# First weights of a transformer block loaded by k tile: one array of 520 columns in place of chunk loads

## The chip, the cores and the metric

The kernel runs on one core of a Trainium2 chip. Five engines work side by side, each through its own list of instructions in order: TensorE (PE in the profile, with PEld for its weight loads), VectorE (DVE), ScalarE (ACT), GpSimd (POOL) and SyncE (SP). They wait for each other by semaphores. SP issues nearly all DMA transfers; their data is moved by 16 DMA engines. The metric is the device time of one execution in microseconds, as a median of runs.

## The reference

One block: a projection of the normalized input into nine parts, a gated delta rule on four heads, dilated attention on eight heads, an output projection and a gated feed-forward part. S and D are 1024, all in float32.

```python
def reference(x, w_in, conv_w, a_log, dt_bias, onorm_g, rel_bias, w_out, ...):
    h = rmsnorm(x, g_mix_pre[l])
    proj = h @ w_in[l]
    qa, ka, va, gate_a, beta_a, alpha_a, qb, kb, vb = jnp.split(proj, split_at, axis=-1)
    out_a = gated_deltanet(qa, ka, va, gate_a, beta_a, alpha_a, ...)
    out_b = dilated_attention(qb, kb, vb, rel_bias)
    mix = jnp.concatenate([out_a, out_b], axis=-1) @ w_out[l]
    x = x + rmsnorm(mix, g_mix_post[l])
    h = rmsnorm(x, g_ffn_pre[l])
    f = (jax.nn.silu(h @ w_gate[l]) * (h @ w_up[l])) @ w_down[l]
    x = x + rmsnorm(f, g_ffn_post[l])
```

The change touches only the first product, `h @ w_in`, and of it the columns that are computed first: 128 columns of the first key head, 128 of the first query head, 256 of the attention's values (`vb`), and the eight of beta and alpha.

## The kernel before

**Products in three terms.** Every float32 matrix is split into a high half, rounded to the format that PE multiplies fast (`fp32r`), and the low half that is left. A product is three matmuls: high by high, high by low, low by high (`mm3`, line 557). A split of weights is a CAST for the high half (ACT or DVE) and a subtraction, TENSOR_TENSOR, for the low half (DVE or POOL); it stands in `split_sb`, line 568. The input x comes transposed, in tiles of 128 of its 1024 features (a "k tile", 0 to 7) by 512 tokens. `prep_xt` (line 1384) multiplies it by the gain `gT`: ACT makes the high half `hTh`, DVE then makes the low half `hTl`.

**The first projection.** `proj_first` (line 755) runs for the first 512 tokens (`hf` 0) tile by tile over k, as its data comes: for each k tile six matmuls of 512 columns for the two chunks (into two PSUM banks named `pj`) and twelve of 264 columns for the values with beta and alpha (four token tiles, banks named `tp`). For k tiles 0 and 1 the three terms are ordered so that those with `hTl` come late. For the second 512 tokens it runs the two chunks alone, and `proj_v` adds the values. A chunk is 128 columns of `w_in` in an array `[chunk, 128, k tile, 128]`; chunk 4 is the first key head, 0 the first query head, 24 and 25 hold the values (256 columns for four k tiles each), so that a k tile of one chunk is a row of 512 bytes in each partition.

**The loads.** `load_w` (line 653) issues on SP, in this order: the gain, k tile 0 of both chunks (64 KB each), `w_ba` (all of beta's and alpha's weights, 32 KB), the values of k tile 0 (128 KB), x of k tile 1 (256 KB), k tile 1 of both chunks and of the values; then for each pair of k tiles the two chunks (128 KB each for two k tiles), x, and the values of each k tile. x of k tile 0 comes on ACT's own queue. Behind these come `ident`, the token rows `xn` (512 KB each, for the norms) and x for the second half of the tokens. Raw weights have four buffers (`rawS`), split weights sixteen (`wS`), x tiles six, token rows three. The DMA semaphores are eight, used in turn, so that an issue also waits until the transfer eight before it has landed.

**The order.** A scheduler in Python (`Weaver`, line 238) runs the parts of the kernel as strands, estimates times, and writes each engine's instructions in the order that it finds. Every instruction is issued from its line 287, which is why the profile shows L287 everywhere. `prep_w` (line 720) is the strand that splits the weights of one chunk; `ev_w` (line 715) names the event that tells `proj_first` that a k tile of a chunk is split. `norm_in` (line 1410) squares a token row on ACT into `ss`, and DVE and POOL make `rtok`, the factor of the norm, of it; PE then transposes `rtok` against `ident`, and `v_sink` (line 838) scales the finished values.

Of the kernel before, what the change touches and what calls it, by code (L numbers as in the profile page):

```python
# [21 lines left out]
P = 128  # L22
# [3 lines left out]
KT = D // P  # L26
# [517 lines left out]
def block_kernel(ctx: ExitStack, tc: tile.TileContext, a, out):  # L544
# [108 lines left out]
    def load_w():  # L653

        yield SY.dma_start(gT[:], a["g_mix_pre_t"])
        first = chunks(order[0]) + chunks(order[1])
        vs = chunks(order[2])
        got = {c: [] for c in first + vs}
        evs = {c: [[Event() for _ in range(2 + (c in first and not i))] for i in range(2)] for c in first + vs}
        for k in range(0, KT, 2):  # L660
            i, j = k // 4, k % 4
            for n, c in enumerate(first):
                if not j:
                    wr = yield rawS.get([P, 4, P], F32, name="wr")
                    got[c].append(wr)
                x = 2 if k else 1
                yield SY.dma_start(got[c][i][:, j:j + x, :], a["w_in"][c][:, k:k + x, :])
                evs[c][i][len(evs[c][i]) - 2 + j // 2 if k else 0].fire()
                if not k:
                    w.spawn(prep_w(c, got[c], evs[c]), 1)  # L670
                if k and not n:
                    yield from load_xt(k, 0)
            if not k:
                yield SY.dma_start(wba[:], a["w_ba"])
            c = vs[i]
            wr = yield rawS.get([P, 4, P], F32, name="wr")
            got[c].append(wr)
            for n in range(2):
                if n:
                    yield from load_xt(k + 1, 0)  # L680
                    for d in first if not k else ():
                        yield SY.dma_start(got[d][0][:, 1:2, :], a["w_in"][d][:, 1:2, :])
                        evs[d][0][1].fire()
                yield SY.dma_start(wr[:, 2 * n:2 * n + 2, :], a["w_in"][c][:, 2 * (j + n):2 * (j + n) + 2, :])
                evs[c][j // 2][n].fire()
                if not j and not n:
                    w.spawn(prep_w(c, got[c], evs[c]), 1)
        yield SY.dma_start(ident[:], a["c_ident"])
        for t in range(3):
            yield from load_x(t)  # L690
            yield from load_xt(t, 1)
        for k in range(3, KT):
            yield from load_xt(k, 1)
            if k == 4:
                yield from load_x(3)
        for t in range(4, NT):
            yield from load_x(t)
        ev_x.fire()
        for item in order[3:]:
            yield from load_item(item)  # L700

    def load_item(item):
        for c in chunks(item):
            z, evs = [], [[Event()] for _ in range(2)]
            for i in range(2):
                wr = yield rawS.get([P, 4, P], F32, name="wr")
                yield SY.dma_start(wr[:], a["w_in"][c][:, 4 * i:4 * i + 4, :])
                z.append(wr)
                evs[i][0].fire()
            w.spawn(prep_w(c, z, evs), 1)  # L710

    ev_x = Event()
    ev_wh = {(c, (i, j)): Event() for c in loaded for i in range(2) for j in range(3)}

    def ev_w(c, k):
        if c in (24, 25):
            return ev_wh[c, (k % 4 // 2, k % 2)]
        return ev_wh[c, (0, min(k, 2)) if k < 4 else (1, k % 4 // 2)]

    def prep_w(c, raw, got):  # L720
        hi, lo = [], []
        for i in range(4):
            if c in (24, 25):
                z = yield wS.get([P, 2, WB], F32R, name="w")
            else:
                z = yield wS.get([P, 4, P], F32R, name="w")
            (lo if i % 2 else hi).append(z)
        wts[c] = hi, lo
        for i, (wh, wl) in enumerate(zip(hi, lo)):
            yield got[i][0]  # L730
            wr = raw[i]
            if c in (24, 25):

                k = 4 * (c - 24) + 2 * i
                yield After(wba[:])
                yield from split_sb(wh[:, :, 256:], wl[:, :, 256:], wba[:, k:k + 2, :])
                wh, wl, wx = wh[:, :, 0:256], wl[:, :, 0:256], wr[:].rearrange("p (k x) c -> p k (x c)", x=2)
            else:
                wh, wl, wx = wh[:], wl[:], wr[:]
            for j, ev in enumerate(got[i]):  # L740
                yield ev
                n, m = wx.shape[1], len(got[i])
                x = slice(*((0, 1, 2, n)[j:j + 2] if m == 3 else (n // m * j, n // m * (j + 1))))
                x = (slice(None), x)
                yield After(wx[x], part=m > 1)
                if c == chunks(order[0])[0] and not i and not j:
                    yield V.tensor_copy(wh[x], wx[x])
                    yield V.tensor_tensor(wl[x], wx[x], wh[x].bitcast(F32), ALU.subtract)
                else:
                    yield from split_sb(wh[x], wl[x], wx[x])  # L750
                ev_wh[c, (i, j)].fire()
            rawS.put(wr)
        loaded[c].fire()

    def proj_first(hf, sinks):

        cs = chunks(order[0]) + chunks(order[1])
        ps = []
        for _ in cs:
            z = yield pj.get([P, 512], F32, name="pj")  # L760
            ps.append(z)
        vs = []
        if not hf:
            for t in range(4):
                z = yield pt.get([P, 4, P], F32, name="tp")
                vs.append(z)
        for k in range(KT):
            if vs and k < 2:
                for c in cs:
                    yield ev_w(c, k)  # L770
                yield ev_xt[k, hf]
                o0, o1 = (mm3(z[:], wh[0][:, k, :], wl[0][:, k, :], *h_of(k, 0, 512), k == 0, False)
                          for z, (wh, wl) in zip(ps, (wts[c] for c in cs)))
                yield [o0[0], o0[2], o1[0], o0[1], o1[1], o1[2]]
            for c, z in zip(cs, ps) if not vs or k > 1 else ():
                yield ev_w(c, k)
                yield ev_xt[k, hf]
                wh, wl = wts[c]
                yield mm3(z[:], wh[k // 4][:, k % 4, :], wl[k // 4][:, k % 4, :], *h_of(k, hf * 512, 512),
                          k == 0, k == KT - 1)  # L780
            if vs:
                yield ev_w(24 + k // 4, k)
                ops = [v_ops(0, t, v_rows(0, z), [k]) for t, z in enumerate(vs)]
                if k < 2:
                    yield [op for o in ops for op in (o[0], o[2])] + [o[1] for o in ops]
                else:
                    for o in ops:
                        yield o
        if hf:
            wS.slots = wS.slots[:8]  # L790
            for c in cs:
                wS.put(*wts[c][0], *wts[c][1])
# [132 lines left out]
        return t  # L925

    convw = const("convw", [P, 12, 4], a["conv_w"])
    wba = pl.tile([P, KT, 8], F32, name="wba")
    bp = pl.tile([P, 8, NT], F32, name="bp")
    dtb = const("dtb", [P, GH], a["dt_bias"].partition_broadcast(P))  # L930
    alog = const("alog", [P, GH], a["a_log"].partition_broadcast(P))
# [441 lines left out]
    with ExitStack() as s0:  # L1373
# [10 lines left out]
        def prep_xt(k, hf, x):  # L1384
# [4 lines left out]
            f = gT[:, k:k + 1]  # L1389
            yield A.activation(hi, x[:], AF.Copy, scale=f)  # L1390
            if not k and not hf:
                yield ev_w(chunks(order[0])[0], 0)
# [1135 lines left out]
def _layout(inp):  # L2528
# [8 lines left out]
        "w_ba": np.ascontiguousarray(w[:, 2048:2056].reshape(KT, P, 8).transpose(1, 0, 2)),  # L2537
# [31 lines left out]
```

## Time and profile before

| | |
|---|---|
| time, median of 3 runs | 1199.91 us (1199.58 to 1201.13) |
| the profiled execution | 1200.32 us |
| its span, first to last instruction | 1198.4 us |
| mean granted clock of TensorE | 0.999 |
| POOL | 160.1 us busy, 13% of the span |
| DMA | 192.51 MB, 161 GB/s in the mean |

The profile is of one execution. Its page gives the busy time of each engine as a share of the span, the chain of work that ended last, and groups of instructions. Other views used below: the timeline (start, length, engine, operation, out<-in, shape, how many in a row; in brackets the idle time of the engine just before and what ended it), and the busy time by stretch (a stretch, its length, then for PE, PEld, DVE, ACT and POOL the busy time and number of instructions, then the granted clock, the share of the DMA engines and GB/s). SPq rows are transfers that SP issues; a start there is the time of the issue, not of the landing.

### The profile page before, as it was taken

The numbers are of one execution on the slowest core, as the hardware profiler recorded it, in microseconds if no ns is written. First come the engines' busy times: TensorE is split into PE (matmuls) and PEld (weight loads), VectorE is DVE, ScalarE is ACT, GpSimd is POOL, SyncE is SP. The second block draws the span as 40 slices with busy tenths as digits, with TensorE's granted clock in tenths as the row PEclk, the third lists the DMA queues.
The fourth block names the chain that finished last, engine by engine and source line by source line (L and its number), as shares of the span: only waits on it lengthen the run. The fifth ranks groups of instructions, "written<-read, shape, count | busy, mean of one in ns | idle before, by whom it ended". The sixth has DMA issues, their size and how long they took to land.

```text
span 1198.4 us, 19655 instructions
## 1 busy us (share of the span) xinstructions
PE 1190.3 (99%) x7105; PEld 993.2 (83%) x7105; DVE 892.9 (75%) x1755; ACT 539.8 (45%) x1063; POOL 160.1 (13%) x133
## 2 busy tenths in 40 slices
PE   9999999999999999999999999999999999999997
PEld 8888898888888888888888888888888888888886
DVE  5699859826887866676988786687666868776886
ACT  6635431136777754455643333333333346444541
POOL 0134311011111200111110010011100100001111
PEclk9999999999999999999999999999999999999999
DMA  8645361877465346784444423332233149544335
GB/s 276 206 144 178 126 174 62 176 244 245 149 212 177 109 161 214 238 252 160 153 163 141 132 99 114 132 123 93 66 114 115 64 160 339 200 144 138 98 123 211
DMA packets 153656, 192.51 MB, mean 161 GB/s; under 512 B 30120, under 2 KB 80296, under 8 KB 153560
## 3 DMA queue, kind: packets, MB, share of 16 engines
q1 hardware_dynamic: 149192, 188.91, 49.1%
q10 hardware_dynamic: 4368, 2.36, 0.7%
q8 instruction: 56, 0.92, 0.3%
q14 instruction: 40, 0.33, 0.1%
HBM read 135.36 MB, written 59.66 MB: 163 GB/s over the span
## 4 chain that ended last, share of the span: by engine, by line
PE 98%; DMA 1%; DVE 0%; issue 0%; ACT 0%; DVEq 0%; SPq 0%; POOLq 0%; ACTq 0%
PE bank L287 52%; PE pj L287 24%; PE pw L287 7%; PE tp L287 6%; PE p L287 4%; PE pS L287 2%; PE pV L287 2%; PE pm L287 2%; DMA convw<-in_conv_w 0%; DMA d_v<-vs 0%; PE otp L287 0%; DVE x L287 0%; DVEq L2565 0%; DVE w L287 0%; SPq L287 0%
## 5 line engine op out<-in xcount | busy, mean ns | idle before, releaser
L287 PE MATMUL pj<-hTh,w 128*128 128x512 f32 x768 | 259.7, 400 | 0.0
L287 PEld LDWEIGHTS pj<-hTh,w 128*128 128x128 f32 x768 | 144.2, 188 | 31.3 <-issue 3.4
L287 ACT CAST wbh<-wraw 128x512 fp32r<-128x512 f32 x130 | 80.3, 621 | 197.1 <-PE bank L287 138.8
L287 PE MATMUL pj<-hTl,w 128*128 128x512 f32 x384 | 149.8, 391 | 0.0
L287 DVE TENSOR_TENSOR wbl<-wraw,wbh 128x512 fp32r<-128x512 f32 x131 | 90.6, 693 | 29.7 <-ACT wbh L287 29.3
L287 PE MATMUL bank<-views 128*128 128x512 f32 (+1 forms) x307 | 84.8, 384 | 0.0
L287 PEld LDWEIGHTS pj<-hTl,w 128*128 128x128 f32 x384 | 72.2, 188 | 12.7 <-DVE hTl L287 0.5
L287 POOL TENSOR_TENSOR m<-m,m 128x512 f32<-128x512 f32 x18 | 36.9, 2048 | 281.5 <-DVE r L287 138.2
L287 PE MATMUL bank<-views,dah 128*128 128x512 f32 (+1 forms) x214 | 73.5, 379 | 0.0
L287 PE MATMUL bank<-dbh,views 128*128 128x512 f32 (+1 forms) x201 | 70.3, 380 | 0.0
L287 PEld LDWEIGHTS bank<-views 128*128 128x128 f32 x307 | 57.5, 188 | 11.5
L287 ACT CAST w<-wr 128x512 fp32r<-128x512 f32 (+2 forms) x62 | 34.2, 560 | 39.8 <-PE pj L287 33.5
L287 PE MATMUL bank<-dbh,dah 128*128 128x512 f32 (+1 forms) x129 | 49.1, 381 | 0.0
L287 DVE SCALAR_TENSOR_TENSOR yc<-raw,convw,yc 128x1024 f32<-128x1024 f32 x36 | 48.5, 1348 | 0.4
L287 PEld LDWEIGHTS bank<-views,dah 128*128 128x128 f32 x214 | 40.0, 188 | 7.6
L287 PE MATMUL pw<-woh,mh 128*128 128x512 f32 x112 | 45.0, 402 | 0.0
L287 ACT ACTIVATE Sr<-Sr,mx 128x384 f32<-128x384 f32 (+3 forms) x64 | 38.0, 596 | 14.1 <-DVE mx L287 14.0
L287 PE MATMUL pw<-woh,ml 128*128 128x512 f32 x112 | 43.8, 391 | 0.0
L287 DVE TENSOR_TENSOR w<-wr,w 128x512 fp32r<-128x512 f32 (+2 forms) x52 | 29.9, 590 | 18.5 <-ACT w L287 13.5
L287 PE MATMUL pw<-wol,mh 128*128 128x512 f32 x112 | 43.7, 390 | 0.0
L287 PEld LDWEIGHTS bank<-dbh,views 128*128 128x128 f32 x201 | 37.6, 188 | 7.2
L287 DVE TENSOR_TENSOR m<-bank,m 128x512 f32<-128x512 f32 x44 | 30.0, 684 | 18.2 <-PE bank L287 18.1
(389 smaller groups left out, 3069.0 us busy)
## 6 DMA issues: line engine op xcount, KB each, us to landing
wraw<-in_w_gate SPq DMA_DIRECT2D x52, 256.0 KB
wraw<-in_w_up SPq DMA_DIRECT2D x52, 256.0 KB
wr<-in_w_in SPq DMA_DIRECT2D x48, 256.0 KB
views<-d_hid SPq DMA_DIRECT2D x48, 256.0 KB
db<-in_w_down SPq DMA_DIRECT2D x40, 256.0 KB
da<-d_hid SPq DMA_DIRECT2D x29, 256.0 KB
d_hid<-x SPq DMA_DIRECT2D x22, 256.0 KB
d_hid<-r SPq DMA_DIRECT2D x22, 256.0 KB
```

The lines of the kernel that those rows point to most:

```text
L287: op.fn(*op.args, **op.kw)
```

## The change

The weights of the two first chunks, the values, beta and alpha are put side by side in a new array `w_first` of 520 columns for each k tile: 128 + 128 + 256 + 8. A k tile of it is one load of 260 KB with rows of 2,080 bytes; k tile 0 is loaded in two parts, 256 columns (both chunks) and 264 (values, beta and alpha). `w_in` stays for all later loads. `wba` and its loads and splits are gone. `prep_first` takes the place of `prep_w` for these weights and splits each k tile in two parts, 256 and 264 columns wide. `w2` holds the split weights in sixteen tiles of two k tiles each, and `w_pair` gives `proj_first` the 128 columns of a chunk. `prep_w` keeps the later chunks. The scratch value `ss` of `norm_in` now has four buffers used in turn, where each token tile had its own.

```diff
     def load_w():
 
         yield SY.dma_start(gT[:], a["g_mix_pre_t"])
-        first = chunks(order[0]) + chunks(order[1])
-        vs = chunks(order[2])
...
-        for k in range(0, KT, 2):
-            i, j = k // 4, k % 4
-            for n, c in enumerate(first):
...
-                x = 2 if k else 1
-                yield SY.dma_start(got[c][i][:, j:j + x, :], a["w_in"][c][:, k:k + x, :])
...
-            if not k:
-                yield SY.dma_start(wba[:], a["w_ba"])
...
+        for k in range(KT):
+            if k:
+                yield from load_xt(k, 0)
+            wr = yield rawS.get([P, 512 + 8], F32, name="wr")
+            parts = [(0, 256), (256, 520)]
+            evs = [Event() for _ in parts]
+            for x, y in [(0, 520)] if k else parts:
+                yield SY.dma_start(wr[:, x:y], a["w_first"][k][:, x:y])
+                for e in evs if k else evs[x // 256:x // 256 + 1]:
+                    e.fire()
+                if not x:
+                    w.spawn(prep_first(k, wr, parts, evs), 1)
         yield SY.dma_start(ident[:], a["c_ident"])
...
+    def prep_first(k, raw, parts, got):
+        if not k:
+            for n in range(2):
+                for i in range(0, KT, 2):
+                    for nm in "hl":
+                        w2[n, i, nm] = yield wS.get([P, 2, WB], F32R, name="w")
+            for i in range(2):
+                wts[24 + i] = [[w2[1, 4 * i + j, nm] for j in (0, 2)] for nm in "hl"]
+        for n, ((x, y), ev) in enumerate(zip(parts, got)):
+            yield ev
+            wx = raw[:, x:y]
+            wh, wl = (w2[n, k - k % 2, nm][:, k % 2, 0:y - x] for nm in "hl")
+            yield After(wx, part=not k)
+            if not k and not n:
+                yield V.tensor_copy(wh, wx)
+                yield V.tensor_tensor(wl, wx, wh.bitcast(F32), ALU.subtract)
+            else:
+                yield from split_sb(wh, wl, wx)
+            ev_wf[k, n].fire()
+        rawS.put(raw)
+        if k % 4 == 3:
+            loaded[24 + k // 4].fire()
+
+    def w_pair(n, k):
+        return [w2[0, k - k % 2, nm][:, k % 2, n * P:n * P + P] for nm in "hl"]
...
         for k in range(KT):
+            yield ev_wf[k, 0]
+            yield ev_xt[k, hf]
+            o0, o1 = (mm3(z[:], *w_pair(n, k), *h_of(k, hf * 512, 512), k == 0, k == KT - 1) for n, z in enumerate(ps))
             if vs and k < 2:
...
                 yield [o0[0], o0[2], o1[0], o0[1], o1[1], o1[2]]
...
-    wba = pl.tile([P, KT, 8], F32, name="wba")
...
-            ss = px.tile([P, 1], F32, name="ss%d" % t)
+            ss = px.tile([P, 1], F32, name="ss", bufs=4)
...
+    c = r["w_in"]
+    r["w_first"] = np.stack([np.concatenate([
+        c[4, :, k], c[0, :, k], c[24 + k // 4].reshape(P, 4, 256)[:, k % 4], w[k * P:k * P + P, 2048:2056]], axis=1)
+        for k in range(KT)])
```

On SP, at the start of the program, stood these transfers (`wr` is a buffer of raw weights, `xT` an x tile, `gT` the gain):

```order
L287 DMA gT<-in_g_mix_pre_t 128x8
L287 DMA wr<-in_w_in 128x128 x2
L287 DMA wba<-in_w_ba 128x64
L287 DMA wr<-in_w_in 128x256
L287 DMA xT<-in_x_t 128x512
L287 DMA wr<-in_w_in 128x128 x2
L287 DMA wr<-in_w_in 128x256 x2
```

Now the same place reads:

```order
L287 DMA gT<-in_g_mix_pre_t 128x8
L287 DMA wr<-in_w_first 128x256
L287 DMA wr<-in_w_first 128x264
L287 DMA xT<-in_x_t 128x512
L287 DMA wr<-in_w_first 128x520
```

Four transfers of weights ahead of the first x tile became two, and from there x and weights alternate, one of each for a k tile, up to `ident`.

On DVE, behind five MEMSETs at the start, stood the split of k tile 0 of chunk 4, the low half of x, and the low halves of the other weights of k tile 0 (`w` is a buffer of split weights):

```order
L287 CAST w<-wr 128x128
L287 TENSOR_TENSOR w<-wr,w 128x128
L287 SCALAR_TENSOR_TENSOR hTl<-xT,gT,hTh 128x512
L287 TENSOR_TENSOR w<-wr,w 128x128
L287 TENSOR_TENSOR w<-wba,w 128x2x8
L287 TENSOR_TENSOR w<-wr,w 128x256
```

Now there stands:

```order
L287 CAST w<-wr 128x256
L287 TENSOR_TENSOR w<-wr,w 128x256
L287 SCALAR_TENSOR_TENSOR hTl<-xT,gT,hTh 128x512
L287 TENSOR_TENSOR w<-wr,w 128x264
L287 SCALAR_TENSOR_TENSOR hTl<-xT,gT,hTh 128x512
```

Both chunks of k tile 0 are now split by one CAST and one TENSOR_TENSOR of twice the width ahead of the low half of x; the second `hTl` is that of k tile 1. PE's instructions stand in the order that they had, from the first to the last, and behind the start the other engines' do too.

More of the change, by code (lines that the diff above doesn't have):

```diff
@@ L655, in load_w @@
         yield SY.dma_start(gT[:], a["g_mix_pre_t"])
-        first = chunks(order[0]) + chunks(order[1])
-        vs = chunks(order[2])
-        got = {c: [] for c in first + vs}
-        evs = {c: [[Event() for _ in range(2 + (c in first and not i))] for i in range(2)] for c in first + vs}
-        for k in range(0, KT, 2):
-            i, j = k // 4, k % 4
-            for n, c in enumerate(first):
-                if not j:
-                    wr = yield rawS.get([P, 4, P], F32, name="wr")
-                    got[c].append(wr)
-                x = 2 if k else 1
-                yield SY.dma_start(got[c][i][:, j:j + x, :], a["w_in"][c][:, k:k + x, :])
-                evs[c][i][len(evs[c][i]) - 2 + j // 2 if k else 0].fire()
-                if not k:
[L670 to L673, printed above, removed]
-                yield SY.dma_start(wba[:], a["w_ba"])
[L675 to L687, printed above, removed]
+        for k in range(KT):
[10 more added lines that the diff above has]
+                    w.spawn(prep_first(k, wr, parts, evs), 1)
         yield SY.dma_start(ident[:], a["c_ident"])
@@ L703, in load_item @@
         for c in chunks(item):
-            z, evs = [], [[Event()] for _ in range(2)]
+            z, evs = [], [Event() for _ in range(2)]
             for i in range(2):
@@ L708, in load_item @@
                 z.append(wr)
-                evs[i][0].fire()
+                evs[i].fire()
             w.spawn(prep_w(c, z, evs), 1)
     ev_x = Event()
[L713 to L718, printed above, removed]
+    ev_wf = {(k, i): Event() for k in range(KT) for i in range(2)}
+    w2 = {}
+    def prep_first(k, raw, parts, got):
[22 more added lines that the diff above has]
+        return [w2[0, k - k % 2, nm][:, k % 2, n * P:n * P + P] for nm in "hl"]
     def prep_w(c, raw, got):
@@ L722, in prep_w @@
         for i in range(4):
[L723 to L726, printed above, removed]
+            z = yield wS.get([P, 4, P], F32R, name="w")
             (lo if i % 2 else hi).append(z)
         wts[c] = hi, lo
[L729 to L751, printed above, removed]
+        for wh, wl, wr, ev in zip(hi, lo, raw, got):
+            yield ev
+            yield After(wr[:])
+            yield from split_sb(wh[:], wl[:], wr[:])
             rawS.put(wr)
@@ L755, in proj_first @@
     def proj_first(hf, sinks):
-        cs = chunks(order[0]) + chunks(order[1])
         ps = []
-        for _ in cs:
+        for _ in range(2):
             z = yield pj.get([P, 512], F32, name="pj")
@@ L767, in proj_first @@
         for k in range(KT):
+            yield ev_wf[k, 0]
+            yield ev_xt[k, hf]
+            o0, o1 = (mm3(z[:], *w_pair(n, k), *h_of(k, hf * 512, 512), k == 0, k == KT - 1) for n, z in enumerate(ps))
             if vs and k < 2:
[L769 to L773, printed above, removed]
-                yield [o0[0], o0[2], o1[0], o0[1], o1[1], o1[2]]
[L775 to L780, printed above, removed]
+                yield [o0[0], o0[2], o1[0], o0[1], o1[1], o1[2]]
+            else:
+                yield o0
+                yield o1
             if vs:
-                yield ev_w(24 + k // 4, k)
+                yield ev_wf[k, 1]
                 ops = [v_ops(0, t, v_rows(0, z), [k]) for t, z in enumerate(vs)]
@@ L790, in proj_first @@
             wS.slots = wS.slots[:8]
-            for c in cs:
-                wS.put(*wts[c][0], *wts[c][1])
+            wS.put(*(z for (n, _, _), z in w2.items() if not n))
         evs = [w.spawn(sink(hf, z), 1) for sink, z in zip(sinks, ps)]
@@ L1391, in prep_xt @@
             if not k and not hf:
-                yield ev_w(chunks(order[0])[0], 0)
+                yield ev_wf[0, 0]
             yield V.scalar_tensor_tensor(lo, x[:], f, hi.bitcast(F32), ALU.mult, ALU.subtract)
@@ L2536, in _layout @@
             w[:, 3080:3592].reshape(2, 4, P, 2, 256).transpose(3, 0, 2, 1, 4).reshape(4, P, KT, P)]),
-        "w_ba": np.ascontiguousarray(w[:, 2048:2056].reshape(KT, P, 8).transpose(1, 0, 2)),
         "conv_w": np.ascontiguousarray(inp["conv_w"][0].reshape(4, 12, P).transpose(2, 1, 0)),
```

## The prediction

> **What bounds the kernel now.** The page comes first: how busy TensorE (PE) is, and whose work makes up the chain that ended last.
>
> ```profile
> span 1198.4 us, 19655 instructions
> PE 1190.3 (99%) x7105; PEld 993.2 (83%) x7105; DVE 892.9 (75%) x1755; ACT 539.8 (45%) x1063; POOL 160.1 (13%) x133
> PE 98%; DMA 1%; DVE 0%; issue 0%; ACT 0%; DVEq 0%; SPq 0%; POOLq 0%; ACTq 0%
> ```
>
> PE is the bound: 98% of the chain is its own work. An edit that takes nothing from PE can win only where PE waits. The second view is therefore the busy time by stretch; PE's is the first number behind the length.
>
> ```profile
> 0.00:4.00 4.00, 3.02 (x10) 1.33 (x11) 0.84 (x7) 2.25 (x3) 0.20 (x4) 1.00 0.42 112
> 4.00:44.00 40.00, 40.00 (x243) 35.31 (x241) 19.66 (x48) 28.79 (x62) 4.09 (x8) 1.00 0.92 295
> 44.00:46.00 2.00, 1.65 (x12) 1.22 (x12) 1.83 (x4) 1.96 (x5) 0.97 (x1) 1.00 0.41 118
> 46.00:246.00 200.00, 199.73 (x1399) 169.98 (x1400) 170.50 (x301) 72.95 (x113) 46.31 (x30) 1.00 0.51 141
> ```
>
> Between 46 and 246 us PE is idle for 0.27 us in 200, and the granted clock is 1.00 in all four rows. The changed loads serve the first 28 us. "Busy" hides waits, though, since the ends of matmuls are modelled, so the third view is PE's timeline, read by starts. In order: the first matmul of k tile 0, its first with the low half of x (`hTl`), its first for the values, then the first matmuls of tiles 1 and 2, tile 2's first `hTl`, its next weight, tiles 3 and 4; below these the last chunk matmuls of tile 7 (the first of the pair at 25.07 is the last into the first bank), then the transposes and the value matmul that come late.
>
> ```profile
> 4.21 0.97 PE L287 MATMUL pj<-hTh,w 128*128 128x512 f32 x3
> 5.02 0.63 PE L287 MATMUL pj<-hTl,w 128*128 128x512 f32 x2
> ...
> 5.72 0.36 PE L287 MATMUL tp<-w,hTh 128*128 128x264 f32 x1
> ...
> 7.25 0.86 PE L287 MATMUL pj<-hTh,w 128*128 128x512 f32 x3
> ...
> 10.14 0.39 PE L287 MATMUL pj<-hTh,w 128*128 128x512 f32 x1
> 10.50 0.50 PE L287 MATMUL pj<-hTl,w 128*128 128x512 f32 x1
> 10.84 0.62 PE L287 MATMUL pj<-hTh,w 128*128 128x512 f32 x2
> ...
> 13.21 0.40 PE L287 MATMUL pj<-hTh,w 128*128 128x512 f32 x1
> ...
> 16.05 0.40 PE L287 MATMUL pj<-hTh,w 128*128 128x512 f32 x1
> ...
> 25.07 0.62 PE L287 MATMUL pj<-hTh,w 128*128 128x512 f32 x2
> 25.52 0.39 PE L287 MATMUL pj<-hTl,w 128*128 128x512 f32 x1
> 25.75 0.39 PE L287 MATMUL pj<-hTh,w 128*128 128x512 f32 x1
> ...
> 44.18 0.93 PE L287 MATMUL tp<-ident,rtok 128*128 128x128 f32 x7
> 45.31 0.32 PE L287 MATMUL tp<-ident,rtok 128*128 128x128 f32 x1 [0.21 <-POOL rtok L287]
> 45.77 0.39 PE L287 MATMUL tp<-w,hTh 128*128 128x264 f32 x1
> ```
>
> A tile that waits for nothing takes 16.05 - 13.21 = 2.84 us. Tile 0 takes 3.04, tile 1 2.89, tile 2 3.07, so the start holds 9.00 - 8.52 = **0.48 us** that better loads could give. The second place is 44.18 to 45.77: eight transposes in 1.59 us, where seven take 0.93 with the last one's length; unhindered, eight need about 0.95 to the next start. That place holds **0.64 us**. Nothing else that these loads reach has a gap, so some 1.1 us in 1198 is at stake.
>
> **The loads.** SP issues them, one row per run of equal transfers, and the engines that split the weights show when they land.
>
> ```profile
> 1.18 0.89 SPq L287 DMA_DIRECT2D wr<-in_w_in  x2
> ...
> 2.59 0.54 SPq L287 DMA_DIRECT2D wr<-in_w_in  x1
> 3.17 0.43 SPq L287 DMA_DIRECT2D xT<-in_x_t  x1
> ...
> 15.89 0.33 SPq L287 DMA_DIRECT2D ident<-in_c_ident  x1
> ```
>
> ```profile
> 3.33 0.72 ACT L287 ACTIVATE hTh<-xT,gT 128x512 fp32r<-128x512 f32 x1 [0.57 <-DMA xT<-in_x_t]
> 4.22 0.30 ACT L287 CAST w<-wr 128x128 fp32r<-128x128 f32 x1 [0.17 <-DMA wr<-in_w_in]
> ...
> 5.23 0.41 ACT L287 CAST w<-wr 128x256 fp32r<-128x256 f32 x1 [0.60 <-DMA wr<-in_w_in]
> 6.31 0.72 ACT L287 ACTIVATE hTh<-xT,gT 128x512 fp32r<-128x512 f32 x1 [0.68 <-DMA xT<-in_x_t]
> ...
> 8.93 0.72 ACT L287 ACTIVATE hTh<-xT,gT 128x512 fp32r<-128x512 f32 x1 [0.58 <-DMA xT<-in_x_t]
> ...
> 24.62 1.06 ACT L287 ACTIVATE junk<-xn 128x1024 bf16<-128x1024 f32 x1 [0.37 <-DMA xn<-in_x]
> 25.59 0.19 ACT L287 ACTIVATION_READ_ACCUMULATOR junk<-xn 128x1 f32 x1
> 25.68 0.71 ACT L287 ACTIVATE hTh<-xT,gT 128x512 fp32r<-128x512 f32 x1
> 26.29 1.05 ACT L287 COPY raw<-pj 128x512 f32<-128x512 f32 x2
> ```
>
> ```profile
> 3.50 0.23 DVE L287 CAST w<-wr 128x128 fp32r<-128x128 f32 x1 [2.31 <-DMA wr<-in_w_in]
> 3.77 0.29 DVE L287 TENSOR_TENSOR w<-wr,w 128x128 fp32r<-128x128 f32 x1
> 4.08 0.75 DVE L287 SCALAR_TENSOR_TENSOR hTl<-xT,gT,hTh 128x512 fp32r<-128x512 f32 x1
> ...
> 5.67 0.42 DVE L287 TENSOR_TENSOR w<-wr,w 128x256 fp32r<-128x256 f32 x1 [0.54 <-ACT w L287]
> ...
> 43.44 0.43 DVE L287 CAST w<-wr 128x512 fp32r<-128x512 f32 x1 [3.35 <-DMA wr<-in_w_in]
> ```
>
> The first 64 KB is issued at 1.18 and used at 3.50, the second at 4.22. The 128 KB for the values, issued at 2.59, is used at 5.23, 2.64 later. SP spends about 0.47 us an issue (2.59 less 1.18 is three), and the transfers are small, so the first four tiles wait for issues and not for bytes.
>
> **Tile 0, what is added.** The first transfer is now 128 KB for both chunks, issued at the same 1.18. It lands between 3.5 (as the first 64 KB did) and 4.2 (when both had landed); 1.18 + 2.64 = 3.8 is the row of its own size. I take 3.7, since only x is in flight ahead of it. Then VectorE (DVE) runs in line: CAST at 256 columns, 0.30 (between 0.23 at 128 and 0.43 at 512), TENSOR_TENSOR 0.42, and only then `hTl`, 0.75. With the 0.02 to 0.04 between rows: 3.72, 4.06, 4.50, end 5.25, where it was 4.83. PE followed that end by 0.19, so its `hTl` matmul starts at 5.44 and not 5.02: **+0.42**. The cast's end, 4.02, stays before the end of x's high half (3.33 + 0.72 = 4.05), so PE's first start holds. The values' high half is done by about 4.7 and their low half on DVE by 5.7, before PE asks (6.1 and 7.1); there the earlier landing is hidden.
>
> **Tiles 1 and 2, what is removed.** SP issues fewer transfers: x of tile 1 stands fourth on SP and no longer sixth, at about 2.1 where it was 3.17, so it lands near 2.1 + (6.31 - 3.17) = 5.3. Tile 1's weights, issued 0.47 later, land by about 6. ACT casts them by 6.5 and DVE ends their low half by 7.3; PE asks at 7.66 and 7.9. Tile 2's x landed at 8.93; issued more than 2 us sooner, it is early. So the 0.05 and 0.23 over 2.84 in tiles 1 and 2 go: **-0.28**. Had tile 1's weights needed till 7.7, that would be gone and up to 0.3 more. Tile 3 starts at 13.21 + 0.42 - 0.28 = 13.35. From there every tile was fed already.
>
> **The gap at 44.** What PE waits for there goes back to the last x tile of 512 KB (`xn`) and a square on ACT:
>
> ```profile
> 36.78 0.33 SPq L287 DMA_DIRECT2D xn<-in_x  x1
> ```
>
> ```profile
> 42.80 1.06 ACT L287 ACTIVATE junk<-xn 128x1024 bf16<-128x1024 f32 x1 [2.01 <-DMA xn<-in_x]
> ...
> 45.44 0.28 ACT L287 ACTIVATE bp<-tp,rtok 128x8 f32<-128x8 f32 x1
> ```
>
> ```profile
> 44.29 0.97 POOL L287 TENSOR_TENSOR rtok<-n_m,mhalf 128x1 f32<-128x1 f32 x1 [3.57 <-DVE n_m L287]
> ```
>
> The xn issue waits for a buffer that ACT frees, and ACT is nearly full from 26.29 (the copies of the first half) on. Their inputs are ready at about 25.07 + 0.39 = 25.46 and 25.75 + 0.39 = 26.14, but the first copy stood behind a square that had waited for its `xn` until 24.62, and an `hTh`. SP now gets past these loads earlier: `ident` should leave at 11 to 12 and not 15.89, as a tile's splitting (ACT: 0.72 + 0.41 + 0.41 and the gaps, 1.65 us) sets when one of the four buffers of raw weights comes free. With x and `xn` in place the copies start near 25.8 (the first bank, PE's 0.14 and a handover of 0.2). I count the shift that reaches the xn issue as **-0.45**, between 0 (if something else on ACT holds it) and -0.64 (the whole gap). PE comes 0.14 later by itself and finds POOL and ACT done.
>
> **Sum.** These terms don't add up plainly: the gap at 44 swallows lateness of PE up to its size. PE leaves it at the later of 44.32 + 0.95 = 45.27 and 45.77 - 0.45 = 45.32, so everything behind moves by -0.45, less what ACT may lose: I take -0.35. The dropped adds, casts and TENSOR_TENSORs for beta and alpha (0.17 to 0.20 us each) ran beside PE and count nothing. The profiled execution took 1200.32, its span 1198.4, so 1.92 lies around it: 1198.05 + 1.92 = 1199.97. That execution is 0.41 over the median of the three runs, 1199.91; against the median the forecast is **1199.6**.
>
> **A rule of the skill against the change.** The new rows are 2,080 bytes, and start at multiples of 32. The Trainium skill, "DMA: Bandwidth & Descriptors", section "How a descriptor splits into AXI transactions", says that a descriptor not starting on 256 bytes first fetches from the boundary below, unused bytes costing beats: an estimate from it is 65 to 72 beats for such a row against 64 for 2,048 bytes. No row of this trace has such a start. By that rule a load costs up to an eighth more, the sum stays, and the third rival below stays far off.
>
> **Rivals.** (1) *The wider first split is late and nothing is won.* If the 128 KB lands at 4.2, `hTl` ends at 5.75, tile 0 loses 0.92 and tile 3 starts 0.64 late; the copies on ACT are then held by PE, and the gap at 44 swallows the 0.64. Against: nothing else is queued before it. Time 1199.9. (2) *Both places close*: landing at 3.5 makes the start term +0.22 - 0.28 = -0.06, the gap gives its 0.64; time 1199.2. (3) *Slower: rows of 2,080 bytes move slowly.* PE eats a tile's 528 kB (260 KB of weights, 256 KB of x) in 2.84 us, 186 GB/s; the stretch from 4 to 44 us shows 295. If x moves at 295 (0.89 us), the weights have 1.95 us left, and PE starves once their rows move below 136 GB/s, less than half. At a third of 295 a tile takes 3.6 us: seven tiles lose 0.76 each, 5.3, less the 0.64 swallowed, time 1204.6. Against: that 295 is already a mix of 1 KB and 2 KB rows, and the new ones are the longer. (4) *The change does not free SP* (a buffer or an earlier landing holds the queue as before): the start keeps its +0.42 without the -0.28, and the gap hides it; time 1199.9, told with (1).
>
> **How the numbers follow.** Chances: forecast 0.58, (1) with (4) 0.23, (2) 0.14, (3) 0.05. The bounds of the terms give -0.7 to +0.1 on 1199.91; the three runs lie from 0.33 below their median to 1.22 above. The range is 1199.91 - 0.7 - 0.6 = 1198.6 to 1199.91 + 0.1 + 1.2, rounded up to 1201.3; it leaves out (3). A measurement of this kernel tells about 0.2%, 2.4 us, from no change: under 1197.5 is faster, over 1202.3 slower. All PE waits within reach are 1.1 us, so faster has 0.02 (a wait that the rows don't show), slower 0.05, same 0.93.
>
> **What would show it.** Right: `ident` issued near 11.5; PE's first `hTl` matmul near 5.4 and tile 3 near 13.3; no wait in tile 2; the copies near 25.8; the value matmul of 45.77 near 45.3; later rows moved by the same amount. Wrong: tile 1 starting after 7.8 for its weights; waits on `wr` between 8 and 20 us; a shift that grows behind 46 us, which none of these steps makes.

## The result and the profile after

The changed kernel takes **1216.37 us** (median of 4 runs, 1216.07 to 1216.52) where the kernel before takes 1199.93 beside it (1199.58 to 1201.13): a ratio of 1.0135, 95% interval 1.0117 to 1.0152. That is 16.4 us slower. The forecast was 1199.6, and its range ended at 1201.3.

The page of the changed kernel, its first lines and the shares of the chain:

```profile
span 1214.6 us, 19622 instructions
PE 1206.5 (99%) x7105; PEld 994.5 (82%) x7105; DVE 892.9 (74%) x1747; ACT 539.8 (44%) x1060; POOL 160.4 (13%) x132
PE 98%; DMA 0%; DVE 0%; issue 0%; ACT 0%; DVEq 0%; SPq 0%; POOLq 0%; POOL 0%; ACTq 0%
```

PE has the same 7,105 matmuls and is as full as before, but is busy for 16.2 us more (1206.5 against 1190.3). The same work takes longer. The busy time by stretch says where (columns as before: PE, PEld, DVE, ACT, POOL, granted clock, DMA share, GB/s). Of the kernel before, one late stretch:

```profile
846.00:1046.00 200.00, 200.00 (x884) 165.58 (x883) 148.46 (x233) 81.28 (x142) 16.23 (x8) 1.00 0.44 152
```

Of the changed kernel, the start and the same late stretch:

```profile
4.00:44.00 40.00, 39.69 (x232) 34.78 (x230) 20.19 (x44) 29.36 (x61) 4.92 (x8) 1.00 0.87 295
...
846.00:1046.00 200.00, 200.00 (x869) 162.84 (x868) 142.98 (x224) 77.04 (x135) 16.23 (x8) 1.00 0.45 156
```

In 200 us far behind the changed loads PE completes 869 matmuls and not 884: 230.1 ns each instead of 226.2, at a granted clock of 1.00 in both rows. The same PE instruction, compared by its start in the two traces, is 1.36 us late at 44 us, 0.56 at 45.8, 2.5 at 235, 6.6 at 654, 10.5 at 858 and 16.1 at the end: a loss that grows all the way, in stages whose instructions the change does not touch. The prediction had named "a shift that grows behind 46 us, which none of these steps makes" as the sign that it was wrong.

**Which matmuls are slower.** The groups of that stretch, shapes kept apart (count, busy us, mean ns of one), two of them of each kernel. `T1h` lives in the slots in which `hTh` and `hTl` lay during the projections; `B22h` lives in another pool. First the kernel before, then the changed one:

```profile
L287 PE MATMUL bank<-T1h,wbh 128*128 128x512 f32 x32 | 12.4, 389 | 0.0
...
L287 PE MATMUL bank<-B22h,wbh 128*128 128x512 f32 x32 | 12.4, 389 | 0.0
```

```profile
L287 PE MATMUL bank<-T1h,wbh 128*128 128x512 f32 x32 | 12.7, 395 | 0.0
...
L287 PE MATMUL bank<-B22h,wbh 128*128 128x512 f32 x32 | 12.5, 391 | 0.0
```

The same operation, in the same stretch and at the same clock, differs by the tile that it reads. What the change did to these tiles stands in no view of the profile, but in the addresses that the compiled programs give them (bytes in a partition, and the remainder by 256):

```
tile          before             changed
hTh, first    130816 (rem.   0)  130176 (rem. 128)
T1h           130816 (rem.   0)  130176 (rem. 128)
T4h           179968 (rem.   0)  179328 (rem. 128)
B22h           79616 (rem.   0)   79616 (rem.   0)
w slots       2,048 bytes apart  2,112 bytes apart (the first eight)
wr slots      2,048 bytes        2,080 bytes
```

Each of the four raw slots grew by 32 bytes (520 columns for 512), and each of eight split slots by 64 (264 for 256). The pools are stacked, so everything stacked after them moved by 4 x 32 + 8 x 64 = 640 bytes, two and a half times 256, and the split weights came to lie at remainders of 32 to 224. Of the 4,298 matmuls with 512 columns, 4,275 had both operands at a multiple of 256 before. Now 807 have; 1,245 have only the moving operand off, 339 only the weights, 1,907 both. The names `T1h` and `wbh` stand nowhere in the diff.

Compared matmul by matmul (PE's order is the same), the distances from start to start behind 46 us grow by 15.6 us in sum: by 16.0 at the 4,195 of 512 columns, while the other 2,647 together lose nothing (-0.4).

### The profile page after: what moved, and what is told of

Read it like the earlier page. It is cut to its first block, busy times and chain, and to the rows that moved or that the text cites. A ratio compares the mean times of both kernels' runs of the same rounds, so it can differ in the third digit from the quotient of the medians.

```text
span 1214.6 us, 19622 instructions
## 1 busy us (share of the span) xinstructions
PE 1206.5 (99%) x7105; PEld 994.5 (82%) x7105; DVE 892.9 (74%) x1747; ACT 539.8 (44%) x1060; POOL 160.4 (13%) x132
## 4 chain that ended last, share of the span: by engine, by line
PE 98%; DMA 0%; DVE 0%; issue 0%; ACT 0%; DVEq 0%; SPq 0%; POOLq 0%; POOL 0%; ACTq 0%
PE bank L287 52%; PE pj L287 24%; PE pw L287 7%; PE tp L287 6%; PE p L287 4%; PE pS L287 2%; PE pV L287 2%; PE pm L287 1%; DMA xT<-in_x_t 0%; PE otp L287 0%; DVE x L287 0%; DVEq L2540 0%; SPq L287 0%; ACT jk L287 0%; DVE w L287 0%
## 5 line engine op out<-in xcount | busy, mean ns | idle before, releaser
L287 PE MATMUL pj<-hTh,w 128*128 128x512 f32 x768 | 263.0, 404 | 0.3 <-DVE w L287 0.3
```

The source lines that it names most:

```text
L287: op.fn(*op.args, **op.kw)
```

## The experiments

**Theory 1**: the matmuls of 512 columns are slower where an operand does not start at a multiple of 256 bytes; the loads have nothing to do with the 16 us. (Which places cost how much is narrowed further below.) **Theory 2**: the new loads are to blame, by their rows of 2,080 bytes or what they do to other transfers.

### The changed loads, with every operand back at a multiple of 256

`a_aligned` keeps the loads and the order. Raw slots get 2,304 bytes, the split slots of the chunks 2,048. To make room, the first projection uses three raw buffers of its four, and two scratch values share a tile.

```diff
+        four, rawS.slots = rawS.slots, rawS.slots[:3]
...
-            wr = yield rawS.get([P, 512 + 8], F32, name="wr")
+            wr = yield rawS.get([P, 512 + 64], F32, name="wr")
...
-                        w2[n, i, nm] = yield wS.get([P, 2, WB], F32R, name="w")
+                        w2[n, i, nm] = yield wS.get([P, 2, WB if n else 256], F32R, name="w")
```

> Theory 1 (where the operands of the matmuls stand in SBUF): in the changed kernel the raw and split weights have slots of 2,080 and 2,112 bytes, which moves x, the weights and all later tiles of that side off multiples of 256 bytes, and PE then takes about 230 ns a matmul of 512 columns where it took 226.7. Here the loads and each engine's order are those of the changed kernel, but all slots are multiples of 256 bytes again (raw 2,304, split chunks 2,048; the raw weights use three buffers in the first projection, so that this fits). Expected 1199.9 plus what the start loses, 0.9 (tile 3 starts 1.2 us late and the gap at 44 us takes some back): 1200 to 1201.2, and 226.7 ns a matmul between 846 and 1046 us. Theory 2 (the loads, the DMA rows of 2,080 bytes or the clock slow PE): about 1216, as the changed kernel.

`c_512` also aligns, and takes the eight columns of beta and alpha out of the rows again: rows of 2,048 bytes, `wba` in its own load.

```diff
-            wr = yield rawS.get([P, 512 + 8], F32, name="wr")
-            parts = [(0, 256), (256, 520)]
+            wr = yield rawS.get([P, 512], F32, name="wr")
+            parts = [(0, 256), (256, 512)]
...
+            if not k:
+                yield SY.dma_start(wba[:], a["w_ba"])
```

> The change without its eight last columns: rows of 512 columns, the weights of beta and alpha in one load of their own as before, raw slots of 2,048 bytes, split chunks 2,048; all operands at multiples of 256. Theory 1: 1199.5 to 1201.2 (the start as in the changed kernel or a little better). Theory 2: about 1216 if the larger loads cause it, 1200 if the rows of 2,080 bytes do.

Measured: `a_aligned` **1200.39** (11 runs, ratio 1.0002, 0.9993 to 1.0011), `c_512` **1200.18** (11 runs, 0.9999, 0.999 to 1.0008), the kernel before 1200.15 beside them. The whole loss is gone while every load of the change is still there, and theory 2 falls. The two agree within their intervals, so the longer rows cost nothing that shows. In `a_aligned` the late stretch and the groups read as before the change:

```profile
846.00:1046.00 200.00, 200.00 (x884) 165.66 (x883) 148.39 (x231) 80.29 (x141) 15.72 (x8) 1.00 0.44 152
```

```profile
L287 PE MATMUL bank<-T1h,wbh 128*128 128x512 f32 x32 | 12.4, 389 | 0.0
...
L287 PE MATMUL bank<-B22h,wbh 128*128 128x512 f32 x32 | 12.4, 389 | 0.0
```

There `T1h` lies at 130048, 768 bytes off its old place and a multiple of 256: being moved by a multiple of 256 costs nothing.

### The kernel before, with nothing done but a shift

The other half of the proof leaves the loads of before and moves the tiles. `edge` is an unused tile at the bottom of the stack, and a smaller one shifts all that is stacked on it.

```diff
-    edge = pool(ctx, "edge", 1, side="right").tile([P, 56], F32, name="edge")
+    edge = pool(ctx, "edge", 1, side="right").tile([P, 24], F32, name="edge")
```

> The kernel before, with nothing changed but the unused tile at the end of SBUF, 128 bytes smaller: raw weights, split weights, x and all that later takes their places start 128 bytes past a multiple of 256. Theory 1: slower by 8 to 16 us (1208 to 1216), though no load, no order and no row changed; matmuls of 512 columns near 230 ns. Theory 2: 1199.9, within 0.2%.

Measured: **1210.41** (4 runs, ratio 1.0084, 1.0071 to 1.0098), 10.3 us slower, with the same instructions in the same order. So placement alone, with the loads of before, makes PE slower.

The same edit in the changed kernel (`a_edge`) takes the moving operands back to multiples of 256 and leaves 1,747 weights off.

> The changed kernel with the unused tile at the end 128 bytes smaller: x (hTh, hTl) and what later stands in its place are at multiples of 256 again, while most split weights and raw weights are not (32 to 224 bytes past). Theory 1: between, if both operands of a matmul count: some 1,700 matmuls with weights off by 4 ns each, 7 us, plus 0.9 of the start: 1205 to 1210. If only the moving operand counts: 1201. Theory 2: 1216.

Measured: **1206.96** (ratio 1.0058, 1.0044 to 1.0072). 9.4 us of the 16.4 come back with the moving side.

### Moving operand or weights

Two kernels move one side alone. `b_moving128` puts an unused tile of 128 bytes ahead of the pool `ph` of the `hTh` slots; `b_weights128` has that tile and the smaller `edge` as well, which moves the weights and leaves `ph` where it was.

```diff
+    pad = pool(ctx, "pad", 1, side="right").tile([P, 32], F32, name="pad")
     hS = Slots(pool(ctx, "ph", 1, side="right"), "ph", 8)
```

> The kernel before with an unused 128 bytes behind the pool of the weights: the pool of hTh, hTl and what later takes their slots moves by 128 bytes, the weights stay. In the built program 2,821 of the matmuls of 512 columns then read their moving operand from 128 bytes past a multiple of 256 with weights on a multiple of 256, 293 have both off. Placement theory, from the spacings in the last part of the changed kernel (232.9 ns with the moving operand off, 228.8 with both off, 226.7 with none): 2,821 x 6.2 + 293 x 2.1 = 18 us, 1218 (1212 to 1220). Rival, that only the weights' place counts: 215 + 293 matmuls, 1 to 2 us, 1201 to 1202. Rival, that what counts is the difference of the two places (b_shift128 kept most pairs equal): also 18 us, so this run does not tell that one from the first.

> The kernel before with the pool of the weights moved by 128 bytes and the pool of the moving operands left where it was: 1,755 matmuls of 512 columns have weights off a multiple of 256 and a moving operand on one. Placement theory, from a_edge (6.8 us for some 1,730 such matmuls, 3.9 ns each): 1,755 x 3.9 = 6.9 us, 1207 (1204 to 1209). Rival, that only the moving operand counts: 1200.

Measured: `b_moving128` **1215.75** (1.0131, 1.0116 to 1.0146), 15.7 us over 1200.02; `b_weights128` **1207.93** (1.0067, 1.0052 to 1.0082), 7.9 us over it. Moving either side costs time, so the rivals that only one of them counts are out. The rival that the difference of the two places counts is not: in both runs most of the slowed pairs have unequal remainders. Per matmul the loss is 15.7 us / 3,121 with the moving operand off = 5.0 ns (215 more have the weights alone off, so a little less), and 7.9 us / 1,755 = 4.5 ns for weights alone. The groups of the late stretch, of `b_moving128` and then of `b_weights128`:

```profile
L287 PE MATMUL bank<-T1h,wbh 128*128 128x512 f32 x32 | 12.6, 395 | 0.0
...
L287 PE MATMUL bank<-B22h,wbh 128*128 128x512 f32 x32 | 12.5, 389 | 0.0
```

```profile
L287 PE MATMUL bank<-T1h,wbh 128*128 128x512 f32 x32 | 12.5, 391 | 0.0
L287 PE MATMUL bank<-B22h,wbh 128*128 128x512 f32 x32 | 12.5, 391 | 0.0
```

With the slots of `T1h` moved and the weights in place, `T1h` has 395 and `B22h` keeps its 389. With the weights moved alone, both have 391, though only some buffers of `wbh` lie in the moved pool (12 of the 88 matmuls `T1h`, `wbh` of the whole program read from it). The changed kernel's 395 and 391 are the two effects in one trace. At these prices its 1,245 and 339 single ones make 7.8 us; the other 8.6 would fall on 1,907 pairs with both off, 4.5 ns each. This is an estimate: compared with the same matmuls of the kernel before, the trace has 6.1 ns for the moving operand alone, 3.7 for the weights alone, 4.0 for both at unequal remainders (1,411 pairs) and 2.7 for both at equal ones (293).

### How fine

`b_shift64` and `b_shift32` are `b_shift128` with `edge` at 40 and at 48 columns.

> The same as b_shift128 with a shift of 64 bytes: 1,908 pairs with both operands 64 past, 1,237 with the moving operand alone, 323 with the weights alone. If 256 bytes is what is needed: about the 10 us of b_shift128 again, 1210 (1207 to 1215). If multiples of 64 bytes are enough: 1200.2.

> The same with a shift of 32 bytes, same counts. If 256, 128 or 64 bytes is what is needed: about 10 us, 1210 (1207 to 1216). If multiples of 32 bytes are enough: 1200.2; then the losses of the changed kernel, whose offsets are multiples of 32 too, would have to come from somewhere else.

Measured: **1207.07** for 64 bytes (1.006, 1.0043 to 1.0077) and **1212.01** for 32 (1.0099, 1.0084 to 1.0114). Moving the tiles by a multiple of 32 or of 64 bytes is not free. The cost isn't one number for "off", though: with equal counts of pairs, 64 bytes cost 7.1 us, 128 bytes 10.3 and 32 bytes 12.0, and I had expected the three alike. The mean distance from one matmul's start to the next in the traces, for matmuls of 512 columns followed by another of 512 among the last 3,000, by the remainders of the two operands' addresses; the last column leaves out the few distances over 300 ns, in which PE waited and which weigh more in the short rows:

```
moving, weights   kernel         count   ns, all   ns, up to 300
0, 0              before          2878   227.1     226.8
0, 0              a_aligned       2878   227.2     226.9
128, 0            b_moving128     1431   233.5     233.0
0, 128            b_weights128     444   234.6     233.1
128, 128          b_shift128       612   230.3     229.2
64, 0             b_shift64       1141   229.8     229.8
64, 64            b_shift64        612   229.6     228.5
32, 0             b_shift32       1141   233.2     233.2
32, 32            b_shift32        612   230.5     229.3
```

Each row holds other matmuls, though, so their means can't be set against each other closely. What can be compared is the same matmul in each kernel with itself in the kernel before. This is the mean change of its distance in ns, over the whole trace, for the four largest groups by which operands lie in a pool that was moved (`ph` holds the slots of `hTh` and `T1h`, the weights' pool lies apart from it; distances up to 300 ns; in brackets what is off there):

```
matmuls                      count   b_moving128    b_weights128    b_shift128    b_shift64  b_shift32
one in each pool              1401   4.4 (moving)   4.5 (weights)   0.2 (both)    0.0        0.4
moving in ph, weights outside 1213   6.4 (moving)   0.5 (none)      6.0 (moving)  3.0        6.6
both in ph                     291   2.6 (both)     0.5 (none)      2.4 (both)    2.2        2.6
both outside                   804   0.7 (none)     0.4 (none)      1.4 (none)    1.3        1.5
```

The first row settles the rival for those 1,401 matmuls: either operand moved by itself (128 bytes) costs some 4.4 ns, both moved by the same 32, 64 or 128 bytes cost 0.0 to 0.4. For them it is not the place of one operand but the difference of the two that costs, and theory 1 as worded is too broad. It also explains why `b_shift128` is cheaper than `b_moving128`: 1,401 x 4.2 ns is 5.9 us, near the 5.4 between their losses. The third row is an exception: both operands off by the same amount, and still 2.2 to 2.6 ns. The last row, matmuls whose own operands stay in place, moves by up to 1.5 ns, so smaller differences than that mean little here. In `a_aligned`, with all of these at multiples of 256, the change is 0.0. What sets the price of each pair stays open; no run varies one remainder through all its values.

### One of the two slot sizes

`a_raw_only` is the changed kernel with the split slots back at 2,048 bytes and the raw slots at 2,080.

```diff
-                        w2[n, i, nm] = yield wS.get([P, 2, WB], F32R, name="w")
+                        w2[n, i, nm] = yield wS.get([P, 2, WB if n else 256], F32R, name="w")
```

> The changed kernel with its eight slots of split weights back at 2,048 bytes, so that of the two slot sizes only the one of the raw rows (four slots of 2,080 bytes) stays off. Four times 32 bytes move all that lies below by 128: in the built program 2,910 pairs of 512 columns have the moving operand 128 past a multiple of 256 (1,214 of them with weights on a multiple, 1,696 with weights off it too), 355 the weights alone. Placement theory, at 5.0 ns for a moving operand off (b_moving128: 15.7 us for 3,114) and 4.5 ns for weights off alone (b_weights128: 7.9 us for 1,755): 14.6 + 1.6 = 16 us, 1216 (1213 to 1218), so mending one of the two sizes wins nothing. Rival, that the loss goes with how many of the operands' places are changed: half of after's 16 us, 1208.

Measured: **1216.78** (1.014, 1.0124 to 1.0157): mending one size wins nothing, since the 128 bytes that the other shifts by are as bad as 640. Eight more columns in one kind of buffer, four slots of it, are enough for the whole loss. That the loss would go with the number of changed sizes is out.

### The start, in two parts, and the changed kernel again

`a_split` is `a_aligned` with the first transfer of k tile 0 in two parts of 128 columns.

```diff
-            parts = [(0, 256), (256, 520)]
+            parts = [(0, 256), (256, 520)] if k else [(0, 128), (128, 256), (256, 520)]
```

> a_aligned with the first transfer of k tile 0 in two parts of 128 columns (64 KB each), so that DVE splits 128 columns before hTl, as in the kernel before. Theory: the start of a_aligned is late because tile 0 waits for a transfer and a split of 256 columns: hTl's matmul at 5.98, tile 2 at 11.61. With 128 columns hTl's matmul comes at 5.0 to 5.3; x of tile 1 is issued one issue later, and its latency of 4.8 us may keep tile 1's start where it is (8.3). If so, tile 2 at 11.3 to 11.6, 1200.0 to 1200.4, as a_aligned. Rival, that tile 0 alone made the start late: tile 2 at 10.4 to 10.7, the gap at 44 closes too, and it comes to 1199.6, some 0.5 us under the kernel before, which five rounds can hardly tell.

> The changed kernel as it is, on the same chip as a_split: 1216.4 (1216.0 to 1216.9), so that the distance to a_split is taken on one chip. If the loss belonged to a chip or a run, it would come out elsewhere.

Measured: `a_split` **1200.21** (11 runs, ratio 1.0, 0.9991 to 1.0009), the kernel before 1200.17; the changed kernel **1215.73** (1.0132, 1.0119 to 1.0146). So the loss belongs to no one chip or run, and the split start wins nothing that 11 runs can tell. Its trace met neither expectation: `hTl`'s matmul came at 5.91 and not at 5.0 to 5.3, and tile 2 at 10.94, between the two. Neither expectation counted that PE's first matmuls run at half the later rate, in this trace up to 5.83 us (see the last section); that, and not the width of DVE's split, keeps `hTl`'s matmul late here: DVE ends `hTl` at 5.17. PE's rows for these:

```profile
5.91 0.62 PE L287 MATMUL pj<-hTl,w 128*128 128x512 f32 x2
...
10.94 0.39 PE L287 MATMUL pj<-hTh,w 128*128 128x512 f32 x1
```

No version here beats the kernel before.

## Why the prediction was wrong

**The step that failed** is the first inference, made before any sum: "An edit that takes nothing from PE can win only where PE waits", and with it "Nothing else that these loads reach has a gap, so some 1.1 us in 1198 is at stake." Read backwards, it was also used as a bound on loss: the duration of PE's own instructions was taken as fixed, and only waits were allowed to change. In the sum the matmuls behind 46 us thus had a change of nothing, for which no reason was given; they measured 15.6 us. But the change lists two buffers with new sizes, and a buffer's size sets the address of all that is stacked after it. I costed the transfers, casts and subtractions that touch those 520 columns and not the place of the tiles that don't. The third rival, the slower one, was a loss by "rows of 2,080 bytes" on their way in; the rows were harmless (`a_aligned`), their slots were not. It had 0.05, and its 1204.6 was neither the mechanism nor the size.

**The rule on rows.** The prediction weighed the Trainium skill, "DMA: Bandwidth & Descriptors", section "How a descriptor splits into AXI transactions": unaligned starts of rows cost beats. No run here shows such a cost: `a_aligned` with these rows and `c_512` without them lie 0.21 us apart, within their intervals. (Its "No row of this trace has such a start" is not quite so: the rows of the gain `gT`, 8 columns, are 32 bytes.) The Trainium skill, "SBUF — State Buffer", section "Operand start alignment", requires a multiple of the element's size and says that its runs timed nothing. All addresses here meet that rule, and the traces add a price: 227 ns against 228 to 233.

**The steps on the loads**, point by point. SP's queue in the changed kernel (start of the issue, length, transfer), then what ACT and DVE wait for in tile 1:

```profile
1.18 0.89 SPq L287 DMA_DIRECT2D wr<-in_w_first  x2
2.11 0.43 SPq L287 DMA_DIRECT2D xT<-in_x_t  x1
2.58 0.54 SPq L287 DMA_DIRECT2D wr<-in_w_first  x1
...
12.23 0.43 SPq L287 DMA_DIRECT2D ident<-in_c_ident  x1
```

```profile
5.76 0.41 ACT L287 CAST w<-wr 128x264 fp32r<-128x264 f32 x1 [1.54 <-DMA wr<-in_w_first]
6.88 0.72 ACT L287 ACTIVATE hTh<-xT,gT 128x512 fp32r<-128x512 f32 x1 [0.70 <-DMA xT<-in_x_t]
```

```profile
3.83 0.29 DVE L287 CAST w<-wr 128x256 fp32r<-128x256 f32 x1 [2.64 <-DMA wr<-in_w_first]
4.16 0.43 DVE L287 TENSOR_TENSOR w<-wr,w 128x256 fp32r<-128x256 f32 x1
4.50 0.74 DVE L287 SCALAR_TENSOR_TENSOR hTl<-xT,gT,hTh 128x512 fp32r<-128x512 f32 x1
```

- *Tile 0, the work on DVE*: right. The first 128 KB is used at 3.83 (3.72 in the prediction), `hTl` ends at 5.24 (5.25).
- *SP is freed*: right. x of tile 1 is issued at 2.11 (2.1), `ident` at 12.23 (11.5; it was 15.89).
- *Tile 1's x and weights land earlier*: wrong. The x issued at 2.11 is used at 6.88, 4.77 later, where the transfer issued at 3.17 in the kernel before was used at 6.31, 3.14 later. The 132 KB for the values, issued second of the pair at 1.18, is used at 5.76. I carried the latencies of before over to a queue with more bytes in flight, against my own remark that the first tiles waited "for issues and not for bytes". From 6 to 7 us the DMA share reads 1.02 at 351 GB/s, where it was 0.75 at 207, so the likely reason is that this x now shares them with the transfers issued beside it; no run tests that. An issue one microsecond sooner bought nothing.

PE's rows at the start and at the gap (starts of tile 0, its `hTl`, tiles 1 and 2, tile 3; the transposes of `rtok`; the value matmul that follows):

```profile
4.55 1.48 PE L287 MATMUL pj<-hTh,w 128*128 128x512 f32 x3
5.87 0.63 PE L287 MATMUL pj<-hTl,w 128*128 128x512 f32 x2
...
8.01 0.45 PE L287 MATMUL pj<-hTh,w 128*128 128x512 f32 x1
8.77 0.72 PE L287 MATMUL pj<-hTh,w 128*128 128x512 f32 x2 [0.31 <-DVE w L287]
...
11.50 0.40 PE L287 MATMUL pj<-hTh,w 128*128 128x512 f32 x1
...
14.37 0.39 PE L287 MATMUL pj<-hTh,w 128*128 128x512 f32 x1
...
45.54 1.03 PE L287 MATMUL tp<-ident,rtok 128*128 128x128 f32 x8
46.33 0.49 PE L287 MATMUL tp<-w,hTh 128*128 128x264 f32 x2
```

- *The sum of the start*: tile 3 at 14.37, 1.16 behind its 13.21, where +0.14 was forecast. Tile 1 starts 0.76 late (8.01 for 7.25): 0.34 of it stands already at PE's first start (4.55 for 4.21), and the first three matmuls take 1.48 for 0.97, so that `hTl`'s comes at 5.87 though `hTl` was ready at 5.24. So the wait for DVE, on which the +0.42 rested, was not what held PE; its slow first matmuls were (last section). Tile 1 then takes 3.49 for 2.89, as its x is late and DVE's low half of the weights, begun at 8.30, stands behind it; tile 2 takes 2.87 for 3.07. So the +0.42 measured +0.76 and the -0.28 measured +0.40.
- *The gap at 44*: it closed, but not by the step that was forecast. The eight transposes now run in 0.79 without a wait, and the gap swallowed lateness: 1.36 at 44.18 became 0.56 at 45.77. But the shift of -0.45 that should reach the issue of the last `xn` measured +0.05 (36.83 for 36.78), and ACT's copies came at 26.66, not at 25.8, as they now waited for PE. POOL's last `rtok` began 2.06 sooner all the same (42.23 for 44.29), because that `xn` landed sooner behind its issue: ACT squares it 3.67 after, where it took 6.02. Why it did is not shown.

```profile
36.83 0.33 SPq L287 DMA_DIRECT2D xn<-in_x  x1
```

```profile
42.23 1.06 POOL L287 TENSOR_TENSOR rtok<-n_m,mhalf 128x1 f32<-128x1 f32 x1 [2.17 <-DVE n_m L287]
```

- *The size of that gap* was one execution's. In `b_moving128`, whose loads are those of before, PE has no wait there either:

```profile
44.49 1.03 PE L287 MATMUL tp<-ident,rtok 128*128 128x128 f32 x8
45.28 0.49 PE L287 MATMUL tp<-w,hTh 128*128 128x264 f32 x2
```

Its value matmul stands at 45.28 with nothing won by any load, and the same 0.79 stands in the traces of the other four shifted kernels with those loads. So the 0.64 us that the prediction hoped to recover rests on one trace, and the loads alone don't make it; other executions of the kernel before itself have no trace.

**What the loads alone are worth** is `a_aligned` against before: +0.24 us, with an interval of 0.9993 to 1.0011 on the ratio, where -0.35 was forecast for them. In the trace its PE is 1.26 late at tile 3, with its slow first matmuls lasting to 6.38 us, and 0.46 late behind 45.77, and stays within 0.3 to 0.5 to the end. For the loads the forecast "no change that can be measured" held; for the change as written it didn't.

## What to carry to other kernels

Where a diff changes the size of a buffer, list the addresses of every matmul operand before and after, also of tiles that the diff doesn't name, and keep the slots at multiples of 256 bytes, the one layout that cost nothing in every run here; a loss of some 5 ns on each of some 3,000 matmuls outweighs every wait at stake here. A loss that grows evenly through stages that the change doesn't touch, with PE's order, clock and waits the same, points to what the stages share, and operand placement is one such thing. A gap read from one execution should be found in a second before it carries a term of a sum.

## What the runs showed of the hardware

Matmuls of 512 columns in this format start 226.8 ns apart with both operands at multiples of 256 bytes, and 228.5 to 233.2 apart at the other places that were tried (waits over 300 ns left out). For 1,401 of them, moving either operand alone by 128 bytes costs 4.4 ns, and moving both together 0.2. The price stands partly in the modelled lengths (389 against 391 to 395 ns) and not at all in the granted clock, the waits or the engines' shares, which read as before.

The first matmuls run at about half the later rate, up to a moment that differs from run to run under the same loads. The group of the first three of the changed kernel, in `after_again`:

```profile
4.54 1.21 PE L287 MATMUL pj<-hTh,w 128*128 128x512 f32 x3
```

The same three took 1.48 in the first profile (above), and 0.97 in the kernel before. By their starts the distances are 0.57 and 0.43 us in that first profile, where 0.23 is the later rate. The Trainium skill, "TensorE: Matmul & The Clock Gate", section "What's actually happening", says that PE's clock is halved until a window of activity has passed, and that the end of this varies between runs; the starts fit it (by an estimate from its 1.2 GHz, 512 columns take 0.427 us). By stretch the granted clock reads 1.00 there. One microsecond of the kernel before, then two stretches of the changed one, with 6, 6 (in 2 us) and 4 matmuls:

```profile
4.50:5.50 1.00, 1.00 (x6) 0.70 (x4) 0.63 (x3) 0.40 (x3) 0.00 (x0) 1.00 0.95 266
```

```profile
2.00:4.00 2.00, 2.00 (x6) 0.73 (x5) 0.17 (x1) 1.25 (x3) 0.00 (x0) 1.00 0.91 268
4.50:5.50 1.00, 1.00 (x4) 0.85 (x3) 0.74 (x2) 0.00 (x0) 0.00 (x0) 1.00 0.81 220
```

That 1.00 is no measurement: the trace's list of granted clocks has its first entry, the full clock, at 5.72 us in the changed kernel, 5.11 in `after_again` and 3.86 in the kernel before, and the view counts a stretch without an entry as 1.00. Up to that entry PE's matmuls of 512 columns start 426 to 427 ns apart when nothing holds them, the warm-up ones on `junk` too; behind it, about 230. So the trace agrees with the page. Over all 13 profiles the entry comes at 3.75 to 4.42 us in the six with the loads of before and at 4.07 to 7.01 in the seven with the new ones; whether the loads have a part in that is not shown. With tile 2 at 11.50 in one trace of the changed kernel and 10.84 in the other, some 0.7 us of a start in one profile is no property of the kernel.
